# Norm scales and block sums of x moved into the second feed-forward chunk of a one-core encoder layer

## The chip, the core and the metric

The kernel runs on one NeuronCore of a Trainium2 chip. TensorE (PE; weight loads are shown apart as PEld) multiplies, VectorE (DVE), ScalarE (ACT) and GpSimd (POOL) work on tiles of 128 partitions, and SyncE (SP) issues most of the DMAs. The metric is the time of one execution in microseconds (us), as a median over runs.

## What is computed

One encoder layer on 256 rows of width 2048: a SwiGLU feed-forward (ffn1), a mixer (sparse attention and a spatial gate, with one combined input projection `w_in`) and a second feed-forward (ffn2). Each of the three begins with an RMS norm, and each adds to the residual x.

```python
def rms_norm(t, g):
    y = t * lax.rsqrt(jnp.mean(t * t, axis=-1, keepdims=True) + EPS)
    return y * g
def swiglu(h, w_gate, w_up, w_down):
    return (jax.nn.silu(h @ w_gate) * (h @ w_up)) @ w_down
...
x = x + 0.5 * swiglu(rms_norm(x, norm_ffn1[l]), ffn1_w_gate[l], ffn1_w_up[l], ffn1_w_down[l])
h = rms_norm(x, norm_mix[l]);  proj = h @ w_in[l]
...
x = x + merged @ w_out[l]
x = x + 0.5 * swiglu(rms_norm(x, norm_ffn2[l]), ffn2_w_gate[l], ffn2_w_up[l], ffn2_w_down[l])
```

D_MODEL is 2048 and D_FF is 5632, so a feed-forward has 11 chunks of 512 hidden columns, each with 512 gate and 512 up columns.

## The kernel before

**Products.** Every float32 operand is split into a rounded part and a remainder (`split_to`: a cast on ACT, L226, and a subtraction on DVE, L227), and each product is three matmuls: high by high, low by high, high by low. The x side is `xTh`/`xTl` (x transposed, 16 blocks of 128 columns by 256 rows), the weight side `wh`/`wl`, split on the chip from the loaded tile `w`. A step of the plain `gemm` (L278 to L280) takes one block k: 12 matmuls of 512 columns (two row halves, gate and up, three products each).

**Chunks.** `ffn` computes its first `plain` chunks with `gemm` (two in ffn1, one in ffn2). All later ones go through `gemm_seven` (L318 to L320), which saves one of eight block products in some groups: for a pair of blocks named in `XSEVEN = (0, 3)` it multiplies sums of the x blocks (`xSh`/`xSl`) with sums of weight blocks (`T`, L332 to L341). `x_sums` makes them: one addition `xTh + xTl` of 128x512 (L505), four additions of 128x128 (L483 to L486) and a split. The sums are asked for after the last plain chunk's closing work. That place is called the border here.

**The norm.** `Normed` holds the transposed planes. In ffn1 (`pair`) x arrives in eight pairs of blocks (kp 0 to 7). For kp 0 `first_squares` sums the squares of 256 columns (L419), `prescale` makes a provisional row scale `pre` (POOL, L389), and its reciprocal `undo` (L406). Each pair is then scaled (`scaled`, L411), transposed on PE (L429) and split (`split_pair`: L436 on ACT, L437 on DVE). The provisional scale is removed in `finish`, where `rstd` is multiplied by `undo`. `rstd` itself is applied to the outputs of the chunk (L550, L552 in plain chunks, the Silu and L590 in the others). In the mixer's and ffn2's norm (`pair_turned`) the scaled pair is copied to 16-bit planes (L445), which a DMA transposes; scaling goes by the first 512 columns.

**Order.** The program is written through a scheduler that simulates time lines and sets the order of instructions on each engine. Each engine then runs its own list in order. Side work is put into the deque `pending` (`later`); `tick` takes one stage out after each step k, `flush` takes all. x is loaded pair by pair on SP's queue between the first weight tiles. Raw weight tiles have three buffers, split tiles four of each kind, temporaries (`t`) eight, accumulators six banks, and transposes or extra products (`tr`) two.

Of the kernel before, what the change touches and what calls it, by code (L numbers as in the profile page):

```python
# [21 lines left out]
P = 128  # L22
S = 256
# [43 lines left out]
def block_kernel(ctx: ExitStack, tc: tile.TileContext, x, positions, norm_ffn1, ffn1_w_gate, ffn1_w_up,  # L67
# [43 lines left out]

    const.tile([P, 24], F32, name="pad")
    xres = act.tile([P, NT, D], F32, tag="xres", name="xres")

    def load_x(kp):
# [11 lines left out]

    ident = const.tile([P, P], F32, name="ident")  # L130
    make_identity(nc, ident)
    mhalf = const.tile([P, 8], F32, name="mhalf")
    nc.gpsimd.memset(mhalf, -0.5)
    warm = const.tile([P, 8], F32, name="warm")
# [91 lines left out]
        nc.scalar.copy(hi, src)  # L226
        nc.vector.tensor_sub(lo, src, hi.bitcast(F32))  # L227

    def gemm(xh, xl, nk, load, widths, first=0, rate=1, lead=None):

        ncol = sum(widths)
        kmax = 2048 // ncol
        banks = [[None] * len(widths) for _ in range(NT)]
        k0 = 0
        while k0 < nk:
            kg = min(1 if k0 < first else kmax, nk - k0)
            w = wraw.tile([P, 2048], F32, tag="w", name=uid("w"))
            wv = w[:, :kg * ncol].rearrange("p (k c) -> p k c", k=kg)
            load(k0, kg, wv)
            for kk in range(kg):  # L240
                k = k0 + kk

                offs = []
                o = 0
                for wd in widths:
                    offs.append(o)
                    o += wd
                parts = []
                cur = []
                for j, wd in enumerate(widths):  # L250
                    if cur and offs[j] + wd - offs[cur[0]] > 1024:
                        parts.append(cur)
                        cur = []
                    cur.append(j)
                parts.append(cur)
                hl = {}
                for part in parts:
                    a = offs[part[0]]
                    n = sum(widths[j] for j in part)
                    whi = wsp.tile([P, 1024], F32R, tag="wh", name=uid("wh"))  # L260
                    wlo = wsp.tile([P, 1024], F32R, tag="wl", name=uid("wl"))
                    with ExitStack() as order:
                        if lead is not None and k == 0:
                            for ins in lead:
                                order.enter_context(tc.issue_after(getattr(ins, "ins", ins)))
                        split_to(whi[:, :n], wlo[:, :n], wv[:, kk, a:a + n])
                    for j in part:
                        b = offs[j] - a
                        hl[j] = (whi[:, b:b + widths[j]], wlo[:, b:b + widths[j]])
                for t in range(NT):  # L270
                    sh = xh(k, t)
                    sl = xl(k, t)
                    for j, wd in enumerate(widths):
                        if k == 0:
                            banks[t][j] = bank()
                        o_ = banks[t][j][:, :wd]
                        whj, wlj = hl[j]
                        nc.tensor.matmul(o_, sh, whj, start=(k == 0), stop=False)  # L278
                        nc.tensor.matmul(o_, sl, whj, start=False, stop=False)  # L279
                        nc.tensor.matmul(o_, sh, wlj, start=False, stop=(k == nk - 1))  # L280
                tick(rate)
            k0 += kg
        return banks
# [107 lines left out]
    class Normed:  # L391

        def __init__(self, gi):
            self.gi = gi
            self.h = act.tile([P, KD, S], F32R, tag="xTh", name=uid("xTh"))
            self.l = act.tile([P, KD, S], F32R, tag="xTl", name=uid("xTl"))
            self.ss = small.tile([P, NT, 4], F32, tag="ss", name=uid("ss"))
            self.rstd = small.tile([P, NT], F32, tag="rstd", name=uid("rstd"))  # L400
            self.pre = small.tile([P, NT], F32, tag="pre", bufs=2, name=uid("pre"))
            self.undo = small.tile([P, NT], F32, tag="undo", bufs=2, name=uid("undo"))
# [9 lines left out]
                                     scale=self.pre[:, t:t + 1])  # L412
            return xs

        def first_squares(self):
            ss = stile(2)
            for t in range(NT):
                sq = ttile([P, 256])
                nc.scalar.activation(sq, xres[:, t, 0:256], AF.Square, accum_out=ss[:, t:t + 1])  # L419
            self.prescale(ss, 256)  # L420

        def pair(self, kp):
            tr = trbank([P, 2, S])
            if kp == 0:
                self.first_squares()
            xs = self.scaled(kp)
            for j in range(2):
                for t in range(NT):
                    nc.tensor.transpose(tr[:, j, t * P:(t + 1) * P], xs[:, t, j * P:(j + 1) * P], ident)  # L429
            return self.split_pair(kp, tr)  # L430

        def split_pair(self, kp, tr):
# [20 lines left out]
        def stages(self, c):  # L453
            out = [lambda: self.pair_turned(2 * c), lambda: self.pair_turned(2 * c + 1)]
            out.insert(0 if c == 0 else 2, lambda: self.squares(c))
            if c == 0:
# [36 lines left out]
    def ffn(nrm, wg, wu, wd, after_chunk, first=0, lead=None, plain=1):  # L493
        with tc.tile_pool(name=uid("ffn"), bufs=1) as pool:
# [7 lines left out]
            def x_sums(i):  # L502
                k = 2 * XSEVEN[i]
                f = ttile([P, 2, S])
                nc.vector.tensor_add(f, nrm.h[:, k:k + 2, :].bitcast(F32), nrm.l[:, k:k + 2, :].bitcast(F32))  # L505
# [5 lines left out]
            def xsums(g):  # L511
                i = XSEVEN.index(g)
                return [(xSh[:, i, c, :], xSl[:, i, c, :]) for c in range(4)]

            for f0, nf, nseven in PARTS:
                last_part = f0 + nf == FF // 512
# [17 lines left out]
                for fi in range(nf):  # L534
# [6 lines left out]
                                                  "(k p) c -> p k c", p=P))  # L541
                    fulls = {}
                    if fc < plain:
                        b = gemm(nrm.xh, nrm.xl, KD, load, [512, 512], first=first if fc == 0 else 0,
                                 lead=lead if fc == 0 else None)
                        if fc == plain - 1:
                            flush()
                        for t in range(NT):
                            sg = ttile()
                            nc.scalar.activation(sg, b[t][0], AF.Silu, scale=nrm.rstd[:, t:t + 1])  # L550
# [1 line left out]
                            nc.vector.scalar_tensor_tensor(hh, b[t][1], nrm.rstd[:, t:t + 1], sg,  # L552
                                                           op0=ALU.mult, op1=ALU.mult)
                            later(partial(turn_chunk, fi, t, hh, fulls))
                        if fc == plain - 1:
                            for i in range(len(XSEVEN)):
                                pending.appendleft(partial(x_sums, i))
                            tick(len(XSEVEN))
                    else:

                        e = pool.tile([P, 4, 512], F32, tag="e", name=uid("e"))
# [22 lines left out]
                        for t in range(NT):  # L584
                            sg = ttile()
                            nc.vector.tensor_add(sg, b[t][0], e[:, 2 * t, :])
                            nc.scalar.activation(sg, sg, AF.Silu, scale=nrm.rstd[:, t:t + 1])
                            hh = ttile()
                            nc.vector.tensor_add(hh, b[t][1], e[:, 2 * t + 1, :])
                            nc.vector.scalar_tensor_tensor(hh, hh, nrm.rstd[:, t:t + 1], sg,  # L590
                                                           op0=ALU.mult, op1=ALU.mult)
# [406 lines left out]

    def to_ffn2(c):
        if n2[0] is None:  # L1000
            n2[0] = Normed(2)
        later(*n2[0].stages(c))

    with tc.tile_pool(name="mix", bufs=1) as pool:
# [28 lines left out]
```

## Time and profile before

| what | us |
|---|---|
| median of three runs (2077.43 to 2080.61) | 2079.18 |
| the profiled execution | 2082.29 |
| its span in the trace | 2080.5 |
| PE busy in the span | 2048.1 |
| DVE busy | 1561.3 |
| ACT busy | 1240.1 |

The profiled execution is 3.1 us above the median and 1.8 us above its own span. Rows of the trace count from the start of the span. A row of a timeline has start, duration, engine, line, operation and tiles, and in brackets how long the engine was idle before it and on what that ended. "x4" joins four instructions. Durations of neighbours overlap on PE and DVE, so that the step from one start to the next is what an instruction costs in a row.

### The profile page before, as it was taken

The numbers are of one execution on the slowest core, as the hardware profiler recorded it, in microseconds if no ns is written. First come the engines' busy times: TensorE is split into PE (matmuls) and PEld (weight loads), VectorE is DVE, ScalarE is ACT, GpSimd is POOL, SyncE is SP. The second block draws the span as 40 slices with busy tenths as digits, with TensorE's granted clock in tenths as the row PEclk, the third lists the DMA queues.
The fourth block names the chain that finished last, engine by engine and source line by source line (L and its number), as shares of the span: only waits on it lengthen the run. The fifth ranks groups of instructions, "written<-read, shape, count | busy, mean of one in ns | idle before, by whom it ended". The sixth has DMA issues, their size and how long they took to land.

```text
span 2080.5 us, 25208 instructions
## 1 busy us (share of the span) xinstructions
PE 2048.1 (98%) x9120; PEld 1698.1 (82%) x9120; DVE 1561.3 (75%) x2024; ACT 1240.1 (60%) x1510; POOL 37.5 (2%) x63
## 2 busy tenths in 40 slices
PE   7999999999999999999999999999999999999999
PEld 6878888888888798888888888887888888888887
DVE  5578888878889757877554457568888888788895
ACT  6556765556666766567454445576677555666663
POOL 1000000000000000120000000000000000000000
PEclk9999999999999999999999999999999999999999
DMA  7656766666666677586665557775666666666674
GB/s 230 205 175 198 218 201 214 202 208 211 218 192 215 202 201 225 182 225 191 204 201 201 185 197 217 224 218 183 193 217 218 194 207 209 200 225 216 195 223 152
DMA packets 251533, 426.13 MB, mean 205 GB/s; under 512 B 106664, under 2 KB 108768, under 8 KB 251408
## 3 DMA queue, kind: packets, MB, share of 16 engines
q1 hardware_dynamic: 250880, 423.29, 64.9%
q0 software_dynamic: 528, 1.23, 0.3%
q8 instruction: 71, 1.16, 0.2%
q14 instruction: 54, 0.44, 0.1%
HBM read 398.26 MB, written 2.10 MB: 192 GB/s over the span
## 4 chain that ended last, share of the span: by engine, by line
PE 90%; DMA 4%; DVE 2%; ACT 2%; issue 1%; POOL 0%; SPq 0%; ACTq 0%; DVEq 0%; POOLq 0%
PE acc L278 11%; PE acc L279 11%; PE acc L318 11%; PE acc L280 11%; PE acc L319 11%; PE acc L320 11%; PE tr L318 9%; PE tr L320 9%; PE tr L319 8%; DMA tu<-pl 3%; ACT wh L226 1%; DVE wl L227 1%; DMA xres<-in_x 0%; ACT t L411 0%; ACT pl L445 0%
## 5 line engine op out<-in xcount | busy, mean ns | idle before, releaser
L226 ACT CAST wh<-w 128x1024 fp32r<-128x1024 f32 (+2 forms) x768 | 784.5, 1035 | 595.4 <-PE acc L319 305.2
L227 DVE TENSOR_TENSOR wl<-w,wh 128x1024 fp32r<-128x1024 f32 (+2 forms) x768 | 914.2, 1198 | 262.9 <-ACT wh L226 254.6
L278 PE MATMUL acc<-wh,xTh 128*128 128x512 f32 (+1 forms) x864 | 333.1, 387 | 2.3 <-ACT wh L226 2.2
L279 PE MATMUL acc<-wh,xTl 128*128 128x512 f32 (+1 forms) x864 | 331.9, 385 | 0.0
L280 PE MATMUL acc<-wl,xTh 128*128 128x512 f32 (+1 forms) x864 | 317.0, 384 | 0.6 <-DVE wl L227 0.5
L318 PE MATMUL acc<-wh,xTh 128*128 128x512 f32 x532 | 207.4, 390 | 0.0
L319 PE MATMUL acc<-wh,xTl 128*128 128x512 f32 x532 | 207.4, 390 | 0.0
L320 PE MATMUL acc<-wl,xTh 128*128 128x512 f32 x532 | 193.0, 390 | 0.0
L319 PE MATMUL tr<-wh,xTl 128*128 128x512 f32 x494 | 192.2, 389 | 0.0
L318 PE MATMUL tr<-wh,xTh 128*128 128x512 f32 x494 | 192.2, 389 | 0.0
L278 PEld LDWEIGHTS acc<-wh,xTh 128*128 128x128 f32 x864 | 162.8, 188 | 33.7 <-ACT wh L226 3.7
L280 PEld LDWEIGHTS acc<-wl,xTh 128*128 128x128 f32 x864 | 161.8, 188 | 31.3 <-DVE wl L227 1.3
L279 PEld LDWEIGHTS acc<-wh,xTl 128*128 128x128 f32 x864 | 162.8, 189 | 29.3
L320 PE MATMUL tr<-wl,xTh 128*128 128x512 f32 x494 | 171.2, 389 | 0.0
L227 DVE TENSOR_TENSOR wl<-T,wh 128x1024 fp32r<-128x1024 f32 (+1 forms) x132 | 125.6, 952 | 49.4 <-ACT wh L226 39.8
L226 ACT CAST wh<-T 128x1024 fp32r<-128x1024 f32 (+1 forms) x132 | 110.3, 836 | 80.2 <-PE acc L319 69.2
L318 PEld LDWEIGHTS acc<-wh,xTh 128*128 128x128 f32 x532 | 100.2, 188 | 20.9
L320 PEld LDWEIGHTS acc<-wl,xTh 128*128 128x128 f32 x532 | 100.2, 188 | 20.8
L319 PEld LDWEIGHTS acc<-wh,xTl 128*128 128x128 f32 x532 | 100.1, 188 | 20.7
L318 PE MATMUL acc<-wh,hTh 128*128 128x512 f32 x296 | 115.2, 389 | 0.0
L319 PE MATMUL acc<-wh,hTl 128*128 128x512 f32 x296 | 115.2, 389 | 0.0
L318 PEld LDWEIGHTS tr<-wh,xTh 128*128 128x128 f32 x494 | 92.7, 188 | 19.3
(268 smaller groups left out, 2956.3 us busy)
## 6 DMA issues: line engine op xcount, KB each, us to landing
w<-in_ffn_w_down SPq DMA_DIRECT2D x88, 1024.0 KB, 5.0
w<-in_ffn_w_gate SPq DMA_DIRECT2D x175, 512.0 KB, 3.8
w<-in_ffn_w_up SPq DMA_DIRECT2D x175, 512.0 KB, 4.7
w<-in_w_in SPq DMA_DIRECT2D x72, 1024.0 KB, 5.0
w<-in_w_out SPq DMA_DIRECT2D x16, 1024.0 KB, 5.1
w<-in_w_in SPq DMA_DIRECT2D x16, 552.0 KB, 4.2
w<-in_w_up_attn SPq DMA_DIRECT2D x8, 1024.0 KB, 5.1
w<-in_w_up_sgu SPq DMA_DIRECT2D x8, 1024.0 KB, 5.2
```

The source lines that it names most:

```text
L226: nc.scalar.copy(hi, src)
L227: nc.vector.tensor_sub(lo, src, hi.bitcast(F32))
L278: nc.tensor.matmul(o_, sh, whj, start=(k == 0), stop=False)
L279: nc.tensor.matmul(o_, sl, whj, start=False, stop=False)
L280: nc.tensor.matmul(o_, sh, wlj, start=False, stop=(k == nk - 1))
L318: nc.tensor.matmul(acc[name], sh, wh, start=first, stop=False)
L319: nc.tensor.matmul(acc[name], sl, wh, start=False, stop=False)
L320: nc.tensor.matmul(acc[name], sh, wl, start=False, stop=last)
```

## The change

- **ffn1's norm** no longer scales x before the transposes: `first_squares`, `scaled` and `undo` are gone there, and `pair` transposes `xres` itself. The first two chunks run on unscaled x, and `rstd` is applied to their outputs as before.
- **Rescaling in place.** A new `spread` turns the 256 values of `rstd` into a tile `cols` of 128x256 (two small operations on DVE, two float32 matmuls with a tile of ones, a copy). In the second chunk `rescale(kp)` is traced behind steps 7, 9, 11, 13 and 15 (kp 0 to 4) and after the last step (kp 5 to 7): `apply` adds `xTh` and `xTl` to a temporary, multiplies it with `cols`, and splits it back into the same tiles. Later chunks use a scale of 1.0.
- **Block sums** in ffn1 are made from that temporary for kp 0 and kp 3, without an addition of their own. In ffn2 they are put into `pending` at the start of `ffn`, so that they run inside its plain chunk.
- **The mixer's norm** copies its planes from unscaled `xres`; ffn2's norm keeps its scaling (`scale=True`).
- The tile `pad` grows from 24 to 152 columns, and the scratch area for dynamic DMAs halves.

```diff
         def pair(self, kp):
             tr = trbank([P, 2, S])
-            if kp == 0:
-                self.first_squares()
-            xs = self.scaled(kp)
             for j in range(2):
+                k = kp * 2 + j
                 for t in range(NT):
-                    nc.tensor.transpose(tr[:, j, t * P:(t + 1) * P], xs[:, t, j * P:(j + 1) * P], ident)
+                    nc.tensor.transpose(tr[:, j, t * P:(t + 1) * P], xres[:, t, k * P:(k + 1) * P], ident)
             return self.split_pair(kp, tr)
...
-            nc.scalar.copy(planes, self.scaled(kp).bitcast(U16).rearrange("p t (c h) -> p h t c", h=2))
+            src = self.scaled(kp) if self.scale else xres[:, :, kp * 256:(kp + 1) * 256]
+            nc.scalar.copy(planes, src.bitcast(U16).rearrange("p t (c h) -> p h t c", h=2))
...
-            nc.vector.tensor_mul(self.rstd, self.rstd, self.undo)
+            if self.scale:
+                nc.vector.tensor_mul(self.rstd, self.rstd, self.undo)
+
+        def spread(self):
+            self.cols = const.tile([P, S], F32, name="cols")
+            bk = trbank([P, S])
+            for t in range(NT):
+                d = ttile([P, P])
+                nc.vector.tensor_scalar(d, ident, self.rstd[:, t:t + 1], None, op0=ALU.mult)
+                nc.tensor.matmul(bk[:, t * P:(t + 1) * P], ones, d, start=True, stop=True)
+            nc.vector.tensor_copy(self.cols, bk)
+
+        def apply(self, kp):
+            f = ttile([P, 2, S])
+            hv, lv = self.h[:, 2 * kp:2 * kp + 2, :], self.l[:, 2 * kp:2 * kp + 2, :]
+            nc.vector.tensor_add(f, hv.bitcast(F32), lv.bitcast(F32))
+            nc.vector.tensor_mul(f, f, self.cols[:, None, :].to_broadcast([P, 2, S]))
+            split_to(hv, lv, f)
+            return f
...
+            def rescale(kp):
+                f = nrm.apply(kp)
+                if kp in XSEVEN:
+                    x_sums(XSEVEN.index(kp), f)
+            if nrm.scale:
+                later(*[partial(x_sums, i) for i in range(len(XSEVEN))])
...
+                        turning = fc == plain - 1 and not nrm.scale
+                        behind = 6
+                        def hook(k):
+                            if k >= behind and (k - behind) % 2 == 1:
+                                rescale((k - behind) // 2)
...
+                        if turning:
+                            for kp in range((KD - behind) // 2, KD // 2):
+                                rescale(kp)
...
-                        if fc == plain - 1:
-                            for i in range(len(XSEVEN)):
-                                pending.appendleft(partial(x_sums, i))
-                            tick(len(XSEVEN))
+                        if turning:
+                            scale[0] = [1.0] * NT
...
-    later(n1.finish, small_loads, rope_tables)
+    later(n1.finish, n1.spread, small_loads, rope_tables)
```

What this does to the lists of the engines is shown at three places.

ScalarE from the start of the program, before (`t<-xres` of 256 columns are the squares and the scaling, `tr` a bank of transposes):

```order
L419 ACTIVATE t_113,s_112<-xres 128x256
L419 ACTIVATE t_115,s_112<-xres 128x256
L411 ACTIVATE t_121<-xres,pre_106 128x256 x2
L411 ACTIVATE t_166<-xres,pre_106 128x256 x2
L411 ACTIVATE t_198<-xres,pre_106 128x256 x2
L436 ACTIVATE xTh_102<-tr_111,gT 128x256
L436 ACTIVATE xTh_102<-tr_165,gT 128x256
L436 ACTIVATE xTh_102<-tr_111,gT 128x256
L226 CAST wh_144<-w_141 128x1024
```

and after:

```order
L432 ACTIVATE xTh_104<-tr_113,gT 128x256 x2
L228 CAST wh_134<-w_131 128x1024
L462 ACTIVATE t_348,ss_106<-xres 128x512
L462 ACTIVATE t_350,ss_106<-xres 128x512
L432 ACTIVATE xTh_104<-tr_155,gT 128x256
L228 CAST wh_167<-w_164 128x1024
```

The squares and the scaling are gone; the first split of x and of a weight tile now stands ahead of anything that reads the second pair of x.

VectorE at the end of ffn1's second chunk, before (`wl_980` to `wl_1017` are the third chunk's first weight tiles, L552 closes the second chunk, L505 and L483 to L486 are the block sums):

```order
L227 TENSOR_TENSOR wl_930<-w_910,wh_929 128x1024
L227 TENSOR_TENSOR wl_980<-w_972,wh_979 128x1024
L227 TENSOR_TENSOR wl_992<-T_975,wh_991 128x1024
L227 TENSOR_TENSOR wl_1005<-w_972,wh_1004 128x1024
L552 SCALAR_TENSOR_TENSOR t_947<-acc_640,rstd_105,t_945 128x512
L552 SCALAR_TENSOR_TENSOR t_951<-acc_648,rstd_105,t_949 128x512
L505 TENSOR_TENSOR t_953<-xTh_102,xTl_103 128x512
L227 TENSOR_TENSOR wl_1017<-T_975,wh_1016 128x512
L483 TENSOR_TENSOR t_955<-t_953 128x128
```

and after (`wl_993` to `wl_1030` answer to them, L589 to L552):

```order
L229 TENSOR_TENSOR xTl_105<-t_956,xTh_104 128x512
L229 TENSOR_TENSOR wl_925<-w_921,wh_924 128x1024
L336 TENSOR_TENSOR T_988<-w_985 128x512
L229 TENSOR_TENSOR xSl_126<-t_914,xSh_125 128x512
L229 TENSOR_TENSOR wl_941<-w_921,wh_940 128x1024
L229 TENSOR_TENSOR xTl_105<-t_961,xTh_104 128x512
L337 TENSOR_TENSOR w_985<-w_985 128x512
L229 TENSOR_TENSOR xTl_105<-t_966,xTh_104 128x512
L338 TENSOR_TENSOR T_988<-w_985 128x512
L229 TENSOR_TENSOR wl_993<-w_985,wh_992 128x1024
```

The second block sum is finished ahead of the third chunk's first weight tile, and rewritten x tiles stand between the last weight splits of the second chunk.

ScalarE at ffn2's border, before (`wh_11458` to `wh_11495` belong to the second chunk, L550 is the Silu of the first):

```order
L226 CAST wh_11408<-w_11389 128x1024
L226 CAST wh_11458<-w_11451 128x1024
L226 CAST wh_11470<-T_11454 128x1024
L226 CAST wh_11483<-w_11451 128x1024
L550 ACT_TABLE_LOAD
L550 ACTIVATE t_11424<-acc_11077,rstd_10708 128x512
L550 ACTIVATE t_11428<-acc_11085,rstd_10708 128x512
L226 CAST wh_11495<-T_11454 128x512
L373 COPY pl_11524<-t_11426 128x1024
L226 CAST xSh_11064<-t_11434 128x512
L226 CAST xSh_11064<-t_11443 128x512
```

and after:

```order
L228 CAST wh_11410<-w_11391 128x1024
L228 CAST wh_11442<-w_11435 128x1024
L228 CAST xSh_11048<-t_11270 128x512
L228 CAST wh_11454<-T_11438 128x1024
L228 CAST wh_11467<-w_11435 128x1024
L228 CAST xSh_11048<-t_11298 128x512
L228 CAST wh_11479<-T_11438 128x512
L587 ACT_TABLE_LOAD
L587 ACTIVATE t_11426<-acc_11061,rstd_10692 128x512
L587 ACTIVATE t_11430<-acc_11069,rstd_10692 128x512
```

Both casts of the sums have moved from behind the Silus to ahead of them, among the casts of the second chunk's weights.

## Rows read from the trace of the kernel before

**Rows 1.** The page: TensorE's busy time, and the chain's shares by engine.

```profile
PE 2048.1 (98%) x9120; PEld 1698.1 (82%) x9120; DVE 1561.3 (75%) x2024; ACT 1240.1 (60%) x1510; POOL 37.5 (2%) x63
...
PE 90%; DMA 4%; DVE 2%; ACT 2%; issue 1%; POOL 0%; SPq 0%; ACTq 0%; DVEq 0%; POOLq 0%
```

**Rows 2.** TensorE's waits: for what; total us, times, longest.

```profile
PE acc L318 <- ACT xSh L226: 9.9, 2, 5.0
PE tr L429 <- ACT t L411: 5.5, 2, 3.5
PE tr L429 <- DVE xTl L437: 3.9, 1, 3.9
```

**Rows 3.** Timeline of the start (columns as explained above).

```profile
4.26 0.42 ACT L419 ACTIVATE t<-xres 128x256 f32<-128x256 f32 x1 [2.03 <-DMA xres<-in_x]
...
9.59 0.91 ACT L411 ACTIVATE t<-xres,pre 128x256 f32<-128x256 f32 x2 [2.40 <-DMA xres<-in_x]
...
13.16 0.81 ACT L436 ACTIVATE xTh<-tr,gT 128x256 fp32r<-128x256 f32 x2
...
15.31 1.09 PE L429 MATMUL tr<-ident,t 128*128 128x128 f32 x4 [3.85 <-DVE xTl L437]
...
16.04 0.78 PE L278 MATMUL acc<-wh,xTh 128*128 128x512 f32 x1
...
20.98 0.39 PE L278 MATMUL acc<-wh,xTh 128*128 128x512 f32 x1
...
25.38 0.48 DVE L437 SCALAR_TENSOR_TENSOR xTl<-tr,gT,xTh 128x256 fp32r<-128x256 f32 x1 [4.35 <-ACT xTh L436]
...
26.43 0.60 PE L429 MATMUL tr<-ident,t 128*128 128x128 f32 x4
```

**Rows 4.** Windows: stretch, busy by engine, clock, DMA share, GB/s.

```profile
8.00:16.00 8.00, 2.13 (x9) 1.41 (x9) 1.75 (x4) 4.37 (x9) 0.00 (x0) 1.00 1.00 343
63.00:108.60 45.60, 45.60 (x202) 37.21 (x201) 27.36 (x34) 25.45 (x28) 0.00 (x0) 1.00 0.60 194
108.60:119.75 11.15, 6.19 (x18) 4.61 (x17) 9.45 (x21) 7.28 (x10) 0.00 (x0) 0.69 0.51 142
1414.75:1426.90 12.15, 7.20 (x20) 5.40 (x19) 10.73 (x22) 8.96 (x12) 0.00 (x0) 0.72 0.47 129
```

**Rows 5.** Timeline of ffn1's border.

```profile
108.61 0.39 PE L318 MATMUL acc<-wh,xTh 128*128 128x512 f32 x1
...
109.54 0.68 DVE L505 TENSOR_TENSOR t<-xTh,xTl 128x512 f32<-128x512 f32 x1
...
110.14 0.69 DVE L227 TENSOR_TENSOR wl<-T,wh 128x512 fp32r<-128x512 f32 x1
...
114.42 0.62 ACT L226 CAST xSh<-t 128x512 fp32r<-128x512 f32 x1 [1.13 <-DVE t L486]
...
115.09 1.65 PE L318 MATMUL acc<-wh,xSh 128*128 128x512 f32 x3 [4.96 <-ACT xSh L226]
```

**Rows 6.** Timeline of ffn2's border.

```profile
1420.58 0.62 ACT L226 CAST xSh<-t 128x512 fp32r<-128x512 f32 x1 [0.39 <-DVE t L486]
...
1421.25 1.22 PE L318 MATMUL acc<-wh,xSh 128*128 128x512 f32 x2 [4.95 <-ACT xSh L226]
```

**Rows 7.** Lines by form, 105 to 1430 us, DVE: busy, mean ns, idle before.

```profile
L227 DVE TENSOR_TENSOR wl<-w,wh 128x1024 fp32r<-128x1024 f32 x461 | 559.0, 1219 | 190.1 <-ACT wh L226 185.0 <-PE tr L759 1.5 <-issue 1.0
...
L627 DVE TENSOR_TENSOR xres<-xres,t 128x1024 f32<-128x1024 f32 x4 | 4.9, 1215 | 0.0
...
L483 DVE TENSOR_TENSOR t<-t 128x128 f32<-128x128 f32 x12 | 3.5, 290 | 1.8 <-ACT t L377 1.7
```

**Rows 8.** Timeline around the mixer's norm, 680 to 752 us.

```profile
680.06 3.34 POOL L389 TENSOR_TENSOR pre<-s,mhalf 128x2 f32<-128x2 f32 x1 [647.23 <-DVE s L388]
...
715.21 0.50 PE L320 MATMUL tr<-wl,hTh 128*128 128x512 f32 x1 [0.52 <-DVE wl L227]
...
750.60 0.44 PE L278 MATMUL acc<-wh,xTh 128*128 128x368 f32 x1 [1.11 <-ACT wh L226]
```

More of the change, by code (lines that the diff above doesn't have):

```diff
@@ L110, in flush @@
         tick(len(pending))
-    const.tile([P, 24], F32, name="pad")
+    const.tile([P, 152], F32, name="pad")
     xres = act.tile([P, NT, D], F32, tag="xres", name="xres")
@@ L131, in block_kernel @@
     make_identity(nc, ident)
+    ones = const.tile([P, P], F32, name="ones")
+    nc.gpsimd.memset(ones, 1.0)
     mhalf = const.tile([P, 8], F32, name="mhalf")
@@ L227, in split_to, with gemm @@
         nc.vector.tensor_sub(lo, src, hi.bitcast(F32))
-    def gemm(xh, xl, nk, load, widths, first=0, rate=1, lead=None):
+    def gemm(xh, xl, nk, load, widths, first=0, rate=1, lead=None, hook=None):
         ncol = sum(widths)
@@ L280, in gemm @@
                         nc.tensor.matmul(o_, sh, wlj, start=False, stop=(k == nk - 1))
+                if hook is not None:
+                    hook(k)
                 tick(rate)
@@ L391, in block_kernel, with __init__ @@
     class Normed:
-        def __init__(self, gi):
+        def __init__(self, gi, scale=False):
+            self.scale = scale
             self.gi = gi
@@ L413, in scaled @@
             return xs
[L415 to L420, printed above, removed]
         def pair(self, kp):
             tr = trbank([P, 2, S])
-            if kp == 0:
-                self.first_squares()
-            xs = self.scaled(kp)
             for j in range(2):
+                k = kp * 2 + j
                 for t in range(NT):
-                    nc.tensor.transpose(tr[:, j, t * P:(t + 1) * P], xs[:, t, j * P:(j + 1) * P], ident)
+                    nc.tensor.transpose(tr[:, j, t * P:(t + 1) * P], xres[:, t, k * P:(k + 1) * P], ident)
             return self.split_pair(kp, tr)
@@ L455, in stages @@
             out.insert(0 if c == 0 else 2, lambda: self.squares(c))
-            if c == 0:
+            if c == 0 and self.scale:
                 out.insert(1, lambda: self.prescale(self.ss[:, :, 0], 512))
@@ L500, in ffn, with x_sums @@
             xSl = pool.tile([P, len(XSEVEN), 4, P], F32R, name=uid("xSl"))
-            def x_sums(i):
+            def x_sums(i, f=None):
                 k = 2 * XSEVEN[i]
-                f = ttile([P, 2, S])
-                nc.vector.tensor_add(f, nrm.h[:, k:k + 2, :].bitcast(F32), nrm.l[:, k:k + 2, :].bitcast(F32))
+                if f is None:
+                    f = ttile([P, 2, S])
+                    nc.vector.tensor_add(f, nrm.h[:, k:k + 2, :].bitcast(F32), nrm.l[:, k:k + 2, :].bitcast(F32))
                 block_sums(xSh[:, i], xSl[:, i], f[:, 0, 0:P], f[:, 1, 0:P], f[:, 0, P:S], f[:, 1, P:S])
@@ L513, in xsums @@
                 return [(xSh[:, i, c, :], xSl[:, i, c, :]) for c in range(4)]
+            def rescale(kp):
+                f = nrm.apply(kp)
+                if kp in XSEVEN:
+                    x_sums(XSEVEN.index(kp), f)
+            scale = [[nrm.rstd[:, t:t + 1] for t in range(NT)]]
+            if nrm.scale:
+                later(*[partial(x_sums, i) for i in range(len(XSEVEN))])
             for f0, nf, nseven in PARTS:
@@ L543, in ffn @@
                     if fc < plain:
+                        turning = fc == plain - 1 and not nrm.scale
[3 more added lines that the diff above has]
+                                rescale((k - behind) // 2)
                         b = gemm(nrm.xh, nrm.xl, KD, load, [512, 512], first=first if fc == 0 else 0,
-                                 lead=lead if fc == 0 else None)
+                                 lead=lead if fc == 0 else None, hook=hook if turning else None)
                         if fc == plain - 1:
                             flush()
+                        if turning:
+                            for kp in range((KD - behind) // 2, KD // 2):
+                                rescale(kp)
                         for t in range(NT):
@@ L586, in ffn @@
                             nc.vector.tensor_add(sg, b[t][0], e[:, 2 * t, :])
-                            nc.scalar.activation(sg, sg, AF.Silu, scale=nrm.rstd[:, t:t + 1])
+                            nc.scalar.activation(sg, sg, AF.Silu, scale=scale[0][t])
                             hh = ttile()
                             nc.vector.tensor_add(hh, b[t][1], e[:, 2 * t + 1, :])
-                            nc.vector.scalar_tensor_tensor(hh, hh, nrm.rstd[:, t:t + 1], sg,
-                                                           op0=ALU.mult, op1=ALU.mult)
+                            nc.vector.scalar_tensor_tensor(hh, hh, scale[0][t], sg, op0=ALU.mult, op1=ALU.mult)
                             later(partial(turn_chunk, fi, t, hh, fulls))
@@ L1000, in to_ffn2 @@
         if n2[0] is None:
-            n2[0] = Normed(2)
+            n2[0] = Normed(2, scale=True)
         later(*n2[0].stages(c))
@@ L1021 @@
     nc = bacc.Bacc("TRN2", target_bir_lowering=False, num_devices=1,
-                   dynamic_dma_scratch_size=4096)
+                   dynamic_dma_scratch_size=2048)
     arrays, args = {}, []
```

## Prediction

> **What bounds the kernel now.** I read the page first: TensorE is busy for 2048.1 of 2080.5 us and carries 90% of the chain that ended last [rows 1]. VectorE and ScalarE have room over the whole span, so work that they gain or lose counts only where TensorE waits for it at that moment. The next view is the list of TensorE's waits [rows 2]. It names three places. Two waits for `xSh`, 9.9 us together, are the borders of ffn1 and ffn2, where the third and the second chunk need block sums that are made only then. Two more, 5.5 us for the scaled tiles and 3.9 us for `xTl`, lie at the start. The change aims at all of these, so the question is how much of each place TensorE gets back, and what is late there next.
>
> The windows say what a wait costs beyond its own length [rows 4]. In the second chunk TensorE does 202 matmuls in 45.60 us, 0.226 us each, at clock 1.00. In the 11.15 us from ffn1's border it does 18, which at 0.226 are 4.1 us: 7.1 us are lost, although the wait itself is 4.96 [rows 5]. The difference is the clock, granted at 0.69 there, between its two levels of 1.2 and 2.4 GHz. ffn2's border loses 12.15 - 20 x 0.226 = 7.6 us, with a wait of 4.95 [rows 6] and a clock of 0.72.
>
> **The start.** The timeline shows why the first product comes late [rows 3]. ScalarE's list is in order: it squares the first pair of x at 4.26, waits for the second pair until 9.59 to scale it, then for the third, and only at 13.16 makes the first `xTh`. So TensorE's third group of transposes runs at 15.31, the first product at 16.04, 0.73 us behind it, and step k=1 begins at 20.98, 4.94 us behind that. After the change ScalarE's list has the first two splits of x and the first weight cast ahead of all that reads the second pair. The weight tile is issued ahead of that pair on SP's queue. TensorE's list has two groups of transposes and then the first product, which therefore follows the second pair's arrival, 9.59, by the same 0.73: 10.3. With the same 4.94, k=1 begins at 15.3, plus the third group of transposes, which now lies among these products: 0.60 us (the group at 26.43) to 1.09 (the group at 15.31, at the low clock). That gives 15.9 to 16.4, a gain of 4.6 to 5.1. I take 4.8. What could hold it back is that the squares for 512 columns now stand on ScalarE ahead of the second pair's split. Two squares of 256 columns took 0.42 each, so I take 0.8 us as their bound, and 4.0 as the lower end. The scaling of pairs 3 to 7 also goes, but lay beside running matmuls and is worth nothing.
>
> **ffn1's border.** The block sums move into the second chunk, so the wait and the low clock behind it go: 7.1 us. What is late next is the third chunk's own weights, which VectorE splits at this place (`wl` at 110.14 stands there between the additions [rows 5]). A wait as short as 1.11 us before TensorE's product was met in the mixer [rows 8], so the lower end is 6.0.
> The sums are not free for VectorE. Each rewritten pair costs it an addition (0.68, as L505 at 109.54), a multiplication with a broadcast (the same: the broadcast form L627 takes 1215 ns where the plain one takes 1219 [rows 7]) and a subtraction (0.69): 2.05 us, times eight 16.4. ScalarE pays eight casts of 0.62, 5.0 us, where it works 25.45 of 45.60 [rows 4]. The two sums add 2 x (4 x 0.29 + 0.69) = 3.7 us on VectorE. So by durations VectorE has 27.36 + 16.4 + 3.7 = 47.5 us of work in a chunk of 45.60. But durations overstate it: the addition of 0.68 at 109.54 is followed by the next start at 110.14 [rows 5], a step of 0.60, or 0.88 of the duration. The 20.1 us added then take 17.7, in all 45.1; the order of the changed program leaves the last pair's subtraction behind the border, and the older operations have the same overlap. It just fits, so I book nothing, and take the case in which it doesn't as a rival.
> The Trainium skill, "VectorE: DVE Perf Modes", section "The DRAIN you can't avoid", says that the next operation does not start until the pipe is empty; read on the durations it would make 47.5 us, 1.9 more than the chunk, and the sum would be that of rival A. The trace shows the steps shorter than the durations here, so I go by the steps.
> The in-place writes also add waits: `xTh` of a pair may be rewritten only when this chunk's products with it are done. The hook stands behind steps 7 to 15 and rewrites the pair six steps back, so TensorE has passed it. Queued behind such a write on ScalarE and VectorE are weight splits for later steps, with four buffers of lead.
>
> **ffn2's border.** Here the sums only move: the second sum's cast now stands ahead of the first chunk's Silus on ScalarE, among the next chunk's weight casts. The loss of 7.6 us goes, but the two casts of 0.62 now delay the Silus that free the accumulators by up to 1.24. I take 7.1, with 6.4 and 7.6 as the ends.
>
> **The mixer's norm.** POOL's `pre` (3.34 us at 680.06) and eight pairs of scalings on ScalarE, 0.91 each like the one at 9.59 [rows 3], are gone. TensorE did not wait for them; but around them stand four short gaps, 2.56 us in sum, the first 0.52 and the longest 1.11 [rows 8], which end on weight splits of ScalarE and VectorE. With a freer ScalarE some close; I take half, 1.3. The planes' copies come earlier, and with them their transposing DMAs on SP's queue, ahead of weight loads that they stood behind. One more gap of the longest kind is the lower end: -1.1 to 2.6.
>
> **Small parts.** `spread` puts two float32 matmuls of 128x128 on TensorE. Four transposes of that size took 0.60 to 1.09 [rows 3], so two cost 0.3 to 0.6, taken as 0.3. The memset of `ones`, `pad` and the scratch area lie beside other work; a factor of 1.0 in place of `rstd` costs the same.
>
> **Sum.** 4.8 + 7.1 + 7.1 + 1.3 - 0.3 = 20.0 us; the ends are 4.0 + 6.0 + 6.4 - 1.1 - 0.6 = 14.7 and 5.1 + 7.1 + 7.6 + 2.6 - 0.3 = 22.1. The profiled execution of 2082.29 would become 2062.3 (span 2060.5). It lay 3.1 us above the median, and no term depends on that, so from 2079.18 I forecast **2059.2**, by the ends 2057.1 to 2064.5.
>
> **Rivals.**
> A: VectorE becomes the bound in the second chunk. For it: 47.5 against 45.60 by durations. Against it: the step of 0.60, and that an overrun by 1.9 is less than the wait of 4.96 that it replaces. If the overrun is concentrated at the border and the clock falls again, that border's 7.1 are lost: 2079.18 - 12.9 = 2066.3.
> B, slower: rewriting in place holds TensorE. If a write to a part of `xTh` were ordered against all products that read the tile, each of the eight would hold TensorE for its chain of 0.68 + 0.68 + 0.62 + 0.69 = 2.67 us. With the clock (7.1 lost for a wait of 4.96, a factor of 1.43) that is 3.8, eight times 30.5, against a gain of 20.0: 2089.7. From six holds on it is a loss. Against it: in the first chunk `xTl` of later pairs is written at 25.38 while products run, and TensorE does not wait [rows 3]; and the changed program's order has TensorE waiting in that chunk for weight splits alone.
> C: the start stays bound by the load. For it: the DMA engines are full from 8 to 16 us, at 343 GB/s [rows 4], so products that begin earlier may meet weights that are not there. Against it: the later weight tiles are issued as the split tiles free their buffers, which comes earlier too. It would give the start's 4.8 back at the next steps: 2064.0.
> D: the change doesn't do what it says in ffn2, because the second sum waits for the last squares or copies of the norm and is late all the same. Against it: the order has its cast ahead of the Silus. It loses 7.1: 2066.3.
>
> **How the numbers follow.** The forecast has a chance of 0.75, A 0.10, C 0.06, D 0.03, B 0.06. The time is the forecast's, 2059.2. The range takes in the ends and A, C and D, with a margin for the spread of the runs (some 1.6 us to either side): 2055.5 to 2067.9; only B is left out, and mixtures of two rivals. Faster by over 0.2%, about what a measurement of this kernel can tell from no change, means under 2075.0. The forecast, A, C and D all lie there: 0.94. Of B, 0.02 falls within 0.2% (five or six holds) and 0.04 above.
>
> **What would show it.** The first product at 10.3 and k=1 at 15.9 to 16.4; if instead a gap opens at k=2 to 4 that ends on a DMA, it is C. No TensorE wait on `xSh` in the list of waits, and the windows of both borders at clock 1.00; a wait on `wl` or `wh` at ffn1's border of more than 2 us is A, with VectorE busy without a gap in the second chunk. TensorE waiting inside the second chunk for `xTh` or `xTl` is B. The mixer's four gaps should be fewer. The prediction is wrong if a new wait of several us appears at a place that had none, above all in the second chunk or where the mixer begins.

## The result, and the profile after

The changed kernel takes 2054.64 us (median of four runs, 2054.14 to 2055.26) against 2079.89 (2077.43 to 2081.26) for the kernel before on the same chip: a ratio of 0.988, with a 95% interval of 0.9863 to 0.9897. That is 25.2 us less, faster as forecast, and 5.2 us more than the 20.0 that the sum gave. The forecast started from 2079.18, so the time is 4.6 us below the 2059.2 that it gave, and 0.9 us below the lower end of the range. The profiled execution took 2055.26, with a span of 2053.5.

The page of after, its row of busy times and the chain by engine (before: [rows 1]). In this trace the chain could be followed back only to 956 us, so its shares can't be set beside those of before:

```profile
PE 2039.0 (99%) x9124; PEld 1695.1 (83%) x9124; DVE 1574.2 (77%) x2043; ACT 1230.7 (60%) x1482; POOL 33.8 (2%) x62
...
PE 51%; DMA 1%; ACT 1%; DVE 0%; issue 0%; SPq 0%; DVEq 0%; ACTq 0%
```

TensorE's waits in after (for what; total us, times, longest), which answer to [rows 2]:

```profile
PE tr L425 <- DMA xres<-in_x: 4.5, 2, 3.2
PE tr L141 <- POOL ident masks.py:199: 2.5, 1, 2.5
PE tr L322 <- ACT wh L228: 1.0, 1, 1.0
PE acc L280 <- ACT wh L228: 0.7, 2, 0.3
```

Neither `xSh` nor a scaled tile is in the list. What TensorE still waits for at length is x itself.

Both programs have 8946 products of 512 or 368 columns in their traces, so the n-th of one can be set beside the n-th of the other. How far after is ahead, by the start of the same product, and what each stretch added:

| place | before | after | ahead | added |
|---|---|---|---|---|
| first product | 16.04 | 9.19 | 6.85 | 6.85 |
| behind ffn1's border | 124.13 | 110.18 | 13.94 | 7.1 |
| end of ffn1 | 642.65 | 626.98 | 15.67 | 1.7 |
| behind the mixer's norm | 771.00 | 750.73 | 20.27 | 4.6 |
| behind ffn2's border | 1426.54 | 1398.69 | 27.85 | 7.6 |
| next chunk of ffn2 | 1447.10 | 1420.68 | 26.42 | -1.4 |
| end of ffn2's first part | 1652.43 | 1625.44 | 26.99 | 0.6 |

The two profiled executions differ by 27.03 us and the medians by 25.25, since the one of before lay high. The borders gave about what was forecast. The start gave 6.85 in place of 4.8, the mixer 4.6 in place of 1.3, and 1.7 us came from two places in ffn1 that the forecast had not named (near 306 and 638 us of before; more on them behind the runs).

Timeline of the start of after, which answers to [rows 3]:

```profile
8.45 1.09 PE L425 MATMUL tr<-ident,xres 128*128 128x128 f32 x4 [3.16 <-DMA xres<-in_x]
...
9.19 0.78 PE L280 MATMUL acc<-wh,xTh 128*128 128x512 f32 x1
...
13.91 0.40 PE L280 MATMUL acc<-wh,xTh 128*128 128x512 f32 x1
```

The second pair of x is there at 8.45, not at 9.59 as in the trace of before. The first product follows it by 0.74, close to the 0.73 that the forecast took over. Step k=1 begins at 13.91, where 15.9 to 16.4 was expected.

ffn1's and ffn2's border in after, and a row of the timeline behind the second (before: [rows 4], [rows 5] and [rows 6]):

```profile
102.02:110.18 8.16, 8.16 (x37) 6.76 (x36) 7.75 (x10) 7.45 (x10) 0.00 (x0) 1.00 0.73 196
1380.00:1400.00 20.00, 20.00 (x90) 16.57 (x89) 17.58 (x32) 14.73 (x22) 1.61 (x1) 1.00 0.61 173
```

```profile
1416.46 0.50 PE L322 MATMUL tr<-wh,xTh 128*128 128x512 f32 x1 [0.97 <-ACT wh L228]
```

TensorE is busy through both borders at clock 1.00. The gap of 0.97 at 1416.46, one chunk later, is new: ScalarE's cast of `wh` stands there behind the cast of a block sum of the hidden tiles (`hSh`) and a copy.

### The profile page after: what moved, and what is told of

The parts are those of the page before. It is cut to its first block, busy times and chain, and to the rows that moved or that the text cites. A ratio compares the mean times of both kernels' runs of the same rounds, so it can differ in the third digit from the quotient of the medians.

```text
span 2053.5 us, 25205 instructions
## 1 busy us (share of the span) xinstructions
PE 2039.0 (99%) x9124; PEld 1695.1 (83%) x9124; DVE 1574.2 (77%) x2043; ACT 1230.7 (60%) x1482; POOL 33.8 (2%) x62
## 4 chain that ended last, share of the span: by engine, by line
PE 51%; DMA 1%; ACT 1%; DVE 0%; issue 0%; SPq 0%; DVEq 0%; ACTq 0%
PE acc L282 7%; PE acc L281 7%; PE acc L280 7%; PE acc L324 6%; PE acc L322 6%; PE acc L323 6%; PE tr L322 5%; PE tr L324 5%; PE tr L323 5%; DMA tu<-pl 1%; DMA w<-in_ffn_w_up 0%; ACT wh L228 0%; DVE wl L229 0%; PE tr L959 0%; DVE xres L673 0%
```

## The experiments

Four theories stood against rivals: that the parts add up, each at its own place; that the mixer's part was more than a chance of one execution; that the rescaling is hidden by idle VectorE time; and that the second pair of x lands earlier because of a changed order of loads.

### Single parts put into the kernel before

**The mixer's norm alone.**

```diff
-            nc.scalar.copy(planes, self.scaled(kp).bitcast(U16).rearrange("p t (c h) -> p h t c", h=2))
+            src = self.scaled(kp) if self.scale else xres[:, :, kp * 256:(kp + 1) * 256]
+            nc.scalar.copy(planes, src.bitcast(U16).rearrange("p t (c h) -> p h t c", h=2))
...
-            nm[0] = Normed(1)
+            nm[0] = Normed(1, scale=False)
```

> The kernel before with one part alone: the mixer's norm copies its planes from unscaled rows. The two traces put 4.6 us of the 27.0 gained between 642 and 771 us. Theory M: the scalings and the provisional scale on ScalarE delay weight splits there, so this part alone gives 3 to 5 us (ratio 0.9976 to 0.9986), and the gaps of TensorE between 715 and 781 us, 5.5 in sum, fall under 1.5. Rival N: the profiled execution of before happened to be slow there (it lay 3.1 us above the median), and this part gives 0 to 1.5 us.

Measured: 2074.87 us against 2080.63, a ratio of 0.9971 (0.9959 to 0.9983), 5.8 us. Theory M holds and N falls; the size lies above M's 3 to 5. The window from 690 to 785 us (stretch, busy time of PE, PEld, DVE, ACT and POOL with counts, clock, DMA share, GB/s), first of before and then of this kernel:

```profile
690.00:785.00 95.00, 91.65 (x468) 81.29 (x467) 59.36 (x89) 64.73 (x112) 2.58 (x4) 1.00 0.74 209
```

```profile
690.00:785.00 95.00, 94.33 (x491) 85.89 (x490) 60.71 (x102) 56.84 (x93) 4.53 (x6) 1.00 0.72 218
```

ScalarE has 7.9 us less to do there, and TensorE does 23 more matmuls in the same 95 us. Idle time alone shows only 3.35 us against 0.67. Where I sum what every matmul's step to the next is beyond the usual step of its form (0.227 us for 512 columns, 0.168 for 368), 6.0 us are lost in before and 1.0 here. The end of a matmul in the profile is modelled, so the idle time before the next one shows only a part of the loss.

**The start alone.**

```diff
-            if kp == 0:
-                self.first_squares()
-            xs = self.scaled(kp)
             for j in range(2):
+                k = kp * 2 + j
...
-                    nc.tensor.transpose(tr[:, j, t * P:(t + 1) * P], xs[:, t, j * P:(j + 1) * P], ident)
+                    nc.tensor.transpose(tr[:, j, t * P:(t + 1) * P], xres[:, t, k * P:(k + 1) * P], ident)
...
-    n1 = Normed(0)
+    n1 = Normed(0, scale=False)
```

> The kernel before with one part alone: ffn1's norm transposes unscaled rows; the block sums stay at the border, of unscaled rows, and nothing is rescaled. Theory S: the start does not depend on the rest, first product near 9.2 and step k=1 near 13.9 as in the changed kernel, a gain of 6.5 to 7.1 us (2073). Rival: the second pair of x lands near 9.6 as in the trace of before, since the tile of ones, which changed the order of GpSimd's list, is not there; then the first product is near 10.3 and the gain 5.5 to 6. The recorded forecast was 4.8.

Measured: 2074.47 us against 2080.63, a ratio of 0.9969 (0.9956 to 0.9982), 6.2 us. Neither the theory nor the rival saw what happened. Timeline of its start:

```profile
8.54 1.08 PE L428 MATMUL tr<-ident,xres 128*128 128x128 f32 x4 [3.42 <-DMA xres<-in_x]
...
9.47 1.03 ACT L226 CAST wh<-w 128x1024 fp32r<-128x1024 f32 x1
...
10.56 0.79 PE L278 MATMUL acc<-wh,xTh 128*128 128x512 f32 x1 [0.94 <-ACT wh L226]
```

The second pair is there at 8.5 without the tile of ones, so the rival's cause is wrong. The first product is late all the same, because the scheduler put a square of 512 columns ahead of the first weight cast on ScalarE: in after that cast runs at 7.55. So 1.4 us at the first product hang on that order. Nor are the 6.2 us all of the start: set beside before by products, this trace ends 7.7 us ahead, of which it has 4.5 where k=1 begins, 1.3 from the two places in ffn1, and 1.4 from the mixer's norm, which this part does not change.

**ffn2's sums alone.**

```diff
+            if plain == 1:
+                later(*[partial(x_sums, i) for i in range(len(XSEVEN))])
...
-                        if fc == plain - 1:
+                        if fc == plain - 1 and plain == 2:
                             for i in range(len(XSEVEN)):
                                 pending.appendleft(partial(x_sums, i))
```

> The kernel before with one part alone: ffn2's block sums put into the deque at the start of ffn2. Theory: the border's 7.6 us go, TensorE has no wait for xSh in ffn2, and 1.2 us may come back in the next chunk (the changed kernel has a gap of 1.25 us there): a gain of 6.1 to 7.6 us. Rival D: the second sum is late all the same, gain under 3.

Measured: 2073.96 us against 2080.63, a ratio of 0.9968 (0.9955 to 0.998), 6.7 us. TensorE's only wait for `xSh` left is ffn1's:

```profile
PE acc L318 <- ACT xSh L226: 5.1, 1, 5.1
```

At ffn2's border 7.3 us are gained and 1.1 given back in the next chunk. The theory holds and rival D falls. This kernel has the same lists as before on every engine up to ffn2; so whatever differs earlier is chance. In the mixer's part (680 to 785 us) it loses 5.0 us by steps where before loses 6.0.

**The kernel before, once more.**

> The kernel before, once more, for a second trace. If the gaps in the mixer (5.5 us between 715 and 781) and the landing of the second pair of x (9.56) are of the program, they are here again within 0.5 us; if they vary by execution, they are not.

Measured: 2080.93 us. The mixer loses 6.0 us again. The second pair's landing is not of the program; the same row of ScalarE as the second of [rows 3], and what follows:

```profile
8.42 0.91 ACT L411 ACTIVATE t<-xres,pre 128x256 f32<-128x256 f32 x2 [1.50 <-DMA xres<-in_x]
...
12.28 0.91 ACT L411 ACTIVATE t<-xres,pre 128x256 f32<-128x256 f32 x2 [2.95 <-DMA xres<-in_x]
...
15.97 0.78 PE L278 MATMUL acc<-wh,xTh 128*128 128x512 f32 x1
```

It landed 1.2 us earlier, and the first product came only 0.07 earlier, since ScalarE waits for the third pair as well (12.28).

### Single parts undone or strained in the changed kernel

**The mixer's rows scaled again**, twice.

```diff
-            nm[0] = Normed(1)
+            nm[0] = Normed(1, scale=True)
```

> The changed kernel with one part undone: the mixer's norm scales its rows again. Theory M: 3 to 5 us of the gain are given back (2058 to 2060), with TensorE's gaps back between 690 and 760 us. Rival N: under 1.5 us.

Measured: 2056.47 us (2053.25 to 2058.22), a ratio to before of 0.9888 (0.9871 to 0.9904): 1.8 us slower than the changed kernel. Since that lies between the two theories, it was run again beside the changed kernel.

> The changed kernel with the mixer's rows scaled again, in more rounds. The part alone gave 5.8 us, undoing it in three rounds 1.8. Theory V: the scalings cost TensorE gaps whose size varies by execution, about 2 us more than the unscaled mixer in the mean; then 2056 to 2057.5 with a spread of some 4 us, against a spread of 1 us of the changed kernel. Rival: the part is worth the same 5 us in both surroundings and the three rounds missed it; then 2058.5 to 2060.5.

> The changed kernel once more, as the measure for the other kernels of this call. 2054.0 to 2055.5 us; first product 9.1 to 9.4, TensorE's lost time in the mixer about 1.2 us.

Measured: 2056.08 us (2055.13 to 2057.11) beside 2054.15 (2053.47 to 2054.79) for the changed kernel: 1.9 us. Theory V has the size right; the spread this time was 2 us, so that part of it isn't confirmed. The window of the first of the two, to be set beside those above:

```profile
690.00:785.00 95.00, 92.82 (x480) 83.60 (x480) 58.30 (x105) 63.09 (x109) 4.20 (x6) 1.00 0.72 215
```

By steps from 680 to 785 us, the kernels with scaled rows lose 6.0, 6.0, 5.0 and 4.7 us where they are built on before, and 3.5 and 2.6 here. Those with unscaled rows lose 1.0 (the part alone) and 0.6 to 1.2 (the changed kernel twice, and the others built on it). So the part is worth 5.0 us on before's surroundings, and 1.5 to 2.4 on the changed ones. ffn2's sums alone, with before's lists up to there, show that 1.0 us of that is chance; the start alone loses 1.3 us less than before without touching the mixer. What makes up the rest of the difference stays open.

**Without rescaling.**

```diff
-                f = nrm.apply(kp)
                 if kp in XSEVEN:
-                    x_sums(XSEVEN.index(kp), f)
+                    x_sums(XSEVEN.index(kp))
...
-                        if turning:
-                            scale[0] = [1.0] * NT
...
-    later(n1.finish, n1.spread, small_loads, rope_tables)
+    later(n1.finish, small_loads, rope_tables)
```

> The changed kernel without the rescaling in place: the block sums are made inside the second chunk from unscaled rows (each with its own addition), later chunks apply rstd to their outputs as the first two do. Theory H: the rescaling lies beside TensorE's work and costs nothing but its two small matmuls, so the time is within 1 us of 2054.6, 0.3 to 0.6 lower. Rival A: VectorE is nearly full in the second chunk and the rescaling holds something up; then this is 2 us or more faster.

Measured: 2055.03 us (2054.06 to 2058.09), a ratio to before of 0.9886 (0.9871 to 0.99), the same as the changed kernel within the spread. Windows of ffn1's second chunk, first of after, then of this kernel:

```profile
56.30:102.02 45.72, 45.72 (x202) 37.31 (x201) 42.30 (x66) 30.37 (x37) 0.00 (x0) 1.00 0.62 194
```

```profile
56.30:102.02 45.72, 45.72 (x202) 37.31 (x201) 31.58 (x47) 26.79 (x31) 0.00 (x0) 1.00 0.58 190
```

The rescaling puts 19 more operations and 10.7 us on VectorE within the chunk, and TensorE is busy throughout in both. Theory H holds, within a spread of 4 us: TensorE waits for nothing there, and for the speed the rescaling isn't needed, since the sums can be made from unscaled rows.

The traces do show one effect of the rescaling, later in ffn1. In before ScalarE copies turned hidden tiles right ahead of the weight casts for which TensorE waits; in after the same copy stands two casts earlier. First two rows of before, then the copy in after:

```profile
304.66 1.35 ACT L377 COPY t<-tu 128x1024 uint16<-128x1024 uint16 x1 [1.70 <-DMA tu<-pl]
...
306.97 0.50 PE L318 MATMUL acc<-wh,hSh 128*128 128x512 f32 x1 [0.41 <-ACT wh L226]
```

```profile
286.15 1.37 ACT L381 COPY t<-tu 128x1024 uint16<-128x1024 uint16 x1 [1.41 <-DMA tu<-pl]
```

All eight traces of kernels that rescale gain 0.85 us on the trace of before at this place. The kernel without rescaling has the lists of before there and gains 0.11; before once more and the three single parts, with the same lists, gain 0.1 to 0.4.

**More work on VectorE.**

```diff
-            nc.vector.tensor_add(f, hv.bitcast(F32), lv.bitcast(F32))
+            for _ in range(3):
+                nc.vector.tensor_add(f, hv.bitcast(F32), lv.bitcast(F32))
             nc.vector.tensor_mul(f, f, self.cols[:, None, :].to_broadcast([P, 2, S]))
```

> The changed kernel with two more additions of 128x512 on VectorE for each rewritten pair (the same addition three times): 16 x 0.60 = 9.6 us more in the second chunk. If VectorE has the 4 us or so of room that the steps leave, the border loses 4 to 6 us, and with the low clock up to 8: 2059 to 2063. If it has over 9.6 us of room, the time stays.

Measured: 2061.94 us (2060.38 to 2063.23), a ratio to before of 0.9916 (0.9901 to 0.9931), 7.3 us slower than the changed kernel. Its window behind the chunk, and TensorE's waits:

```profile
102.42:118.66 16.24, 11.82 (x40) 8.00 (x39) 16.24 (x22) 14.78 (x19) 0.00 (x0) 0.90 0.43 128
```

```profile
PE acc L322 <- ACT wh L228: 2.7, 2, 1.9
...
PE acc L324 <- DVE wl L229: 1.8, 2, 1.6
```

VectorE is busy for all of the 16.24 us, and TensorE waits for splits. This is rival A, brought about by 9.6 us of work. The changed kernel has 45.72 - 42.30 = 3.4 us of room in this chunk.

**The sums back at the border**, from rescaled tiles.

```diff
-                f = nrm.apply(kp)
-                if kp in XSEVEN:
-                    x_sums(XSEVEN.index(kp), f)
+                nrm.apply(kp)
...
                         if turning:
+                            for i in range(len(XSEVEN)):
+                                pending.appendleft(partial(x_sums, i))
+                            tick(len(XSEVEN))
                             scale[0] = [1.0] * NT
```

> The changed kernel with ffn1's two block sums back at the border (each with its own addition, from the rescaled tiles). Theory: the border loses its 7.1 us again, with TensorE waiting about 5 us for xSh and a low clock behind: 2061 to 2062. Rival: VectorE has fewer weight splits left to do there than before, so the sums come sooner and under 4 us are lost.

Measured: 2063.2 us (2063.01 to 2064.31), a ratio to before of 0.9922 (0.9905 to 0.9938), 9.1 us slower than the changed kernel run beside it (2054.15). The wait in its timeline:

```profile
111.48 1.65 PE L322 MATMUL acc<-wh,xSh 128*128 128x512 f32 x3 [7.67 <-ACT xSh L228]
```

The direction is the theory's, but the wait is 7.67 against 4.96 in before [rows 5]: a rewritten pair's subtraction, and the next chunk's weight sums, stand between the additions on VectorE. The place of the sums is worth 9 us once the pairs are rewritten in the same chunk, not 7.

### The loads at the start

**The tile of ones later.**

```diff
-    nc.gpsimd.memset(ones, 1.0)
...
+            nc.gpsimd.memset(ones, 1.0)
             bk = trbank([P, S])
```

> The changed kernel with the tile of ones filled only where it is needed, which leaves GpSimd's first instructions as before. Theory O: the order of GpSimd's loads decides when the second pair of x lands, so it lands near 9.6 and the first product comes near 10.3, 1.1 us later than in the changed kernel. Rival: it lands near 8.3 as in the changed kernel, and 9.56 was that one execution.

Measured: 2055.2 us; first product at 9.08, the second pair at 8.2. Theory O falls. This run alone does not decide it, since GpSimd's loads keep the changed kernel's order here too; but the kernels built on before have before's order, and the pair lands at 8.3 to 8.4 in them. In the one trace of before it was late by chance.

**Three small loads later.**

```diff
+        for g in (gq, gk, gki):
+            nc.vector.tensor_copy(g[:, 0:2], n1.rstd)
         nc.gpsimd.dma_start(gq, q_norm.to_broadcast([P, DH]))
```

> The changed kernel with GpSimd's three loads of 160 KB behind the norm, not among the first loads of x and weights. Theory L: the start now waits for the second pair of x alone (wait of 3.2 us), and 160 KB at the 343 GB/s of that stretch are 0.47 us, so it lands near 7.8 and the first product comes 0.4 to 0.5 us earlier, near 8.7; the time falls by as much. Rival: the split of the first weight tile (wh ready at 8.6) is as late, and the first product stays within 0.2 us of 9.2.

Measured: 2053.59 us (2052.84 to 2055.06) beside 2054.15 for the changed kernel: 0.6 us, less than the spread. First the changed kernel's rows (its second trace), then this kernel's:

```profile
9.36 0.78 PE L280 MATMUL acc<-wh,xTh 128*128 128x512 f32 x1
...
14.06 0.39 PE L280 MATMUL acc<-wh,xTh 128*128 128x512 f32 x1
```

```profile
8.51 0.77 PE L282 MATMUL acc<-wh,xTh 128*128 128x512 f32 x1
...
14.11 0.39 PE L282 MATMUL acc<-wh,xTh 128*128 128x512 f32 x1
```

The first product moves the way of theory L, by 0.85 us where 0.4 to 0.5 was expected. But step k=1 begins no earlier: the steps stayed slow until 13.65 here, 5.1 us from the first product, and until 12.45 in the changed kernel, 3.1 us. That length differs between executions of one list too (see the last section), so a trace of each does not show that the later loads caused it. No version that clearly beats the changed kernel came out of these runs.

## Why the prediction was right or wrong, point by point

- **ffn1's border**, 7.1 forecast: right, 7.1 by the table. No wait and no low clock is left. VectorE's work fits, as was said, with more room: 42.30 us of 45.72 were busy, where 45.1 was worked out. That sum put 17.7 us of steps on 27.36 us of busy time; but busy time counts an overlap once already, and in a denser row the older operations overlap with the new ones too (in after the durations in the chunk add up to 47.9 us). One subtraction of the 34 added operations also falls behind the chunk. Rival A did not occur; with 9.6 us more work it did, which shows its mechanism.
- **ffn2's border**, 7.1 forecast: 7.6 at the border and 1.4 lost one chunk later, 6.2 together. The forecast put the loss on the accumulators behind the Silus. It came at a weight cast behind `hSh` instead, and it varies: by steps 1.6 us were lost around there in this trace, 0.9 in the second one of the same kernel, and between 0 and 1.5 in the others built on it.
- **The start**, 4.8 forecast with 4.0 to 5.1: mis-sized, 6.85 by the first product and 7.07 by the start of k=1, where the forecast counts. The chain was right: the second pair of x, then 0.7 us. The step that failed is "follows the second pair's arrival, 9.59". That time was taken from one execution, in which TensorE's first product did not depend on it; the twelve other traces that keep the order of the loads have the landing at 8.2 to 8.6. The rest lies in "with the same 4.94": from the first product to k=1 the changed kernel took 4.72 with the transposes between, since TensorE was back at full steps 3.1 us after its first product (9.19 to 12.31) and not 4.7 (16.04 to 20.75). The 4.94 was one draw as well: three other traces with before's start lists have 4.2 to 4.5, and full steps after 3.1 to 3.6. The squares, feared at 0.8, held nothing back. The low clock that the forecast puts on the group at 15.31 stands in no record of the trace (last section); the steps there are slow.
- **The mixer's norm**, 1.3 forecast with -1.1 to 2.6: mis-sized, and the larger fault: 4.6. The step that failed is the upper end, "2.56 in sum", with the choice of half. The 2.56 are the four longest of seven waits there, 3.2 us by the list; the list counts idle time by modelled ends, and the sum over steps was 6.0. And all but 1.1 of it closed, not half, since ScalarE lost 7.9 us of work there, which the forecast had itself put down as "gone". Undone in the changed kernel the part is worth 1.8 to 1.9 us, inside the forecast's ends; alone on before it gives 5.8. The sum took each part's worth as the same whatever surrounds it, and here it isn't.
- **The sum and the range.** In the traces, 27.0 us against 20.0, the two terms explain 2.1 + 3.3 of the excess, and two places in ffn1 add 1.7, for which the sum had no term. Of these the 0.85 near 306 us go with the rescaling's lists, as shown above. The 0.87 near 638 us are no effect of the change, as far as the runs tell: with one and the same lists there, before once more gains 0.1 and the three single parts and the kernel without rescaling 0.8 to 0.9; the changed kernel's second trace gains 0.2. By the medians the excess is 5.2, since the trace of before lay high. The range took in every bound that was worked out, but two of the bounds were too narrow on the side of the gain. Measured alone on before, three parts give 5.8 + 6.2 + 6.7 = 18.7 us, each with an interval of some 2.5 us to either side; with the table's 7.1 for ffn1's border that is 25.8 against 25.2 for all. So the total adds up, although single places do not.
- **Rivals B, C, D** did not occur: no wait for `xTh` or `xTl` in the second chunk, no wait on a weight load at k=2 to 4, and the sums in time. That it was faster, given 0.94, came true.

## What to carry to other kernels

Price a gap by the steps of the waiting engine's instructions against their usual step, not by the idle time that a list of waits shows, and take the whole of it as the upper end of what relief can give. The time of an event on which nothing waits is one draw: before it becomes the new bound in a sum, give it a spread. The same part can be worth 5.8 us in one surrounding and 1.9 in another, so measure a part both alone and undone before calling its worth known. Set kernels with like lists beside each other before you call a difference chance.

## What was not expected of the hardware

At the start the steps of 128x512 products are 0.43 us, about twice the usual 0.23, while the granted clock of that stretch in the windows reads 1.00. First the window of before from its first product to k=1, then one behind ffn1's border:

```profile
16.04:20.98 4.94, 4.94 (x14) 3.89 (x13) 4.94 (x6) 4.94 (x10) 0.00 (x0) 1.00 0.78 252
```

```profile
112.74:119.56 6.82, 4.47 (x11) 3.50 (x12) 5.12 (x10) 5.35 (x7) 0.00 (x0) 0.50 0.34 73
```

In the second the clock is granted at 0.50 of 2.4 GHz, the level of 1.2, and the steps are 0.43 as well. The 1.00 of the first is no reading: a trace's record of the granted clock has its first entry only at 20.58 us in before and at 12.29 in the changed kernel, and a window counts time without an entry as full. In all fourteen traces that first entry, at 2.4 GHz, lies within 0.2 us of the end of the last slow step. Which level was granted ahead of it no trace records; the steps are like those at 1.2 GHz. So at the start of these programs go by the steps.

How long the slow steps last after the first product varied too: 3.1 us in the two traces of the changed kernel, 4.7 in before and 3.1 to 3.6 in three more traces with its start lists, 5.1 with the loads later, 2.2 and 5.7 at the extremes. What sets it is not settled.
